# The causal mask of an attention stage moved from a TensorE matmul into two masked copies of the gate row

## Chip, cores and metric

One core of a Trainium2 chip runs the whole program in one launch. The metric is device time in microseconds (us) from the first to the last instruction; lower is better. The kernel before takes 1215.36 us, the median of three runs (1215.21 to 1215.37).

## What is computed

One decoder layer for a sequence of 1024 positions and a width of 1024, all float32. The input is modulated, projected, and mixed by two groups of heads: eight "FoX" heads of width 64 (causal softmax attention with a forget gate) and four retention heads of width 128. An output projection, a layer norm, a gated MLP with a short convolution and a second layer norm follow. The change concerns the FoX heads:

```python
cum = jnp.cumsum(log_f, axis=1).transpose(0, 2, 1)        # per head, over positions
s = jnp.einsum('bhqd,bhkd->bhqk', qi, kh) * scale          # qi: one block of 128 queries
s = s + ci[..., None] - cum[:, :, None, :]
s = jnp.where(key_pos[None, :] <= q_pos[:, None], s, -jnp.inf)
p = jax.nn.softmax(s, axis=-1)
o = jnp.einsum('bhqk,bhkd->bhqd', p, vh)
```

The term `ci` is the same for a whole row of the softmax and drops out. What remains is a row of gate sums, one value per key, added to every query's scores, and the causal mask, which matters only in the 128x128 block on the diagonal: key blocks past it are not computed at all.

## The kernel before

**Numbers in pieces.** Float32 products are made of three TensorE matmuls: an operand is split into a high part (a cast on ScalarE, ACT) and a low part (a subtraction on VectorE, DVE), and high x high, high x low and low x high are accumulated in PSUM.

**The stages.** First come the conditioning rows, the retention heads and the v projection of the FoX heads; their instructions are put in order by a scheduler that works with a timeline. This block also computes the gate sums: log_forget at chunk 8 of the 16 chunks of the v projection, cum_forget at chunk 14, cum_store (which writes the sums to the DRAM tensor cum_d) at chunk 15. Then comes the attention stage, 281 to 476 us of the span, with its order of work written out by hand; then the output projection, the layer norm, the MLP.

**The attention stage.** A loop of 64 steps runs over 8 heads x 8 query blocks; the names in the profile carry head and block, so S3_5 is block 5 of head 3. Step (h, i) does this:

- TensorE (PE) makes the scores of query block i against keys 0 to 128(i+1), negated, in PSUM tile ps: one matmul for the high part of q (L796) and one for the low part (L797) per cut of up to 512 keys, both against ks. In the last cut a third matmul (L800) multiplies a bfloat16 identity by a bfloat16 mask (0, or a big number above the diagonal) and so adds the mask to the diagonal block.
- DVE adds the gate row nb (a copy of head h's row of cum_d on all 128 partitions, 512 KB, loaded at L753) and takes the row minimum in the same instruction (L802). ACT takes exp(min - S) with its row sum (L809), DVE the reciprocal (L812), GpSimd (POOL) multiplies S by it (L813).
- Three steps later (LAG) PE transposes S block by block (L835), ACT casts the high part (L841), DVE subtracts for the low part (L842). Four steps later, every other step, PE multiplies by v (L851); ACT and DVE add the result into mixF (L857, L858).
- The q and k projection of the next head is spread over steps 3 to 7 and 0 to 2 (PE L765 to L767, then ACT and DVE L771 to L781, which write qh, ks and ql).

fox_alloc (L750) takes the tiles of a head at step 3 of the head before, nb among them: from the pool X (16 buffers of 4 KB per partition) for the first two heads and from the pool VM after that, where the v tiles of finished heads come free.

**The weights of a head.** fox_w (L636) takes two new tiles of X, loads w_qk of head h into a raw tile (512 KB), casts the high part in one ACT instruction of 128x1024 (L641) and subtracts the low part in two DVE instructions of 128x512 (L644). It is called at step 4, for the head after the next.

**Other work in the stage.** w_out is split in pieces: loaded (park), cast (L990), subtracted (L997) and stored to DRAM (wod, SP L1003); in head 7 the split halves come back as sixteen loads of 512 KB (wo, SP L1009). SyncE (SP) also copies parts of w_down inside DRAM (td, L1112). All these transfers are issued by SP in one order; where one of them must wait for an engine, those behind it in SP's order wait too. Adding DMAs (a DMA that adds to its destination) are issued from POOL's queue; before, the MLP alone has them (L1106).

## Time and profile before

| What | Value |
| --- | --- |
| median of three runs | 1215.36 us (1215.21 to 1215.37) |
| span of the profiled execution | 1214.8 us |
| busy in that span: PE, PEld (weight loads) | 1198.3 us (99%), 1002.4 us (83%) |
| busy: DVE, ACT, POOL | 910.9 us (75%), 653.9 us (54%), 229.0 us (19%) |
| granted clock of TensorE | 0.999 |
| the 64 mask matmuls (L800) | 14.7 us busy, 230 ns each in the median |
| the 64 minima (L802) | 47.4 us busy, 741 ns each in the mean |
| the 8 loads of nb, 512 KB each | 5.1 us from issue to landing in the median |

A row of the profile reads: line, engine, operation, output tile <- input tiles, shape, count, then busy time and the mean of one, then how long the engine had been idle before these instructions and which instruction ended that idle time. In the timeline a row begins with start and length in us. PE's matmuls are pipelined, so that lengths overlap: the next one starts before the last has ended. SPq is SP's queue of DMA issues. The profiled execution has a span of 1214.8 us, 0.56 less than the median of the runs.

### The profile page before, as it was taken

Reading aid. Unit: us, or ns where it says so; the run is one execution under the profiler, and the core shown is the slowest. Engines: PE = TensorE matmul, PEld = TensorE weight load, DVE = VectorE, ACT = ScalarE, POOL = GpSimd, SP = SyncE. Lnnn points to the kernel's source line nnn. Section 1 sums busy time; section 2 is a strip of 40 time slices with the busy share of each in tenths; the row PEclk is TensorE's granted clock in tenths of the full one; section 3 lists DMA queues with packets and bytes.
Section 4 is the critical chain, followed back from the end, with each engine's and each line's share of the span. In section 5 each row is a group of like instructions: output and inputs, shape, how many; then the busy total and the mean of one; then the engine's idle time right before and its main releaser. Section 6 shows DMA issues by size and latency. Waiting matters only on the chain.

```text
span 1214.8 us, 17196 instructions
## 1 busy us (share of the span) xinstructions
PE 1198.3 (99%) x6005; PEld 1002.4 (83%) x6005; DVE 910.9 (75%) x1757; ACT 653.9 (54%) x1201; POOL 229.0 (19%) x274
## 2 busy tenths in 40 slices
PE   8999999999999999999999999999999999999997
PEld 6888888997888888888888888888888888888875
DVE  7847747766888887456988778787787876886586
ACT  6635444345777766567755545455454565543452
POOL 0015335012333333000021323211000010000021
PEclk9999999999999999999999999999999999999999
DMA  9523444605575658223268887776554489875751
GB/s 358 227 87 122 139 148 143 202 32 175 164 222 164 203 171 335 96 77 115 87 178 204 193 223 185 171 184 175 152 139 128 148 249 297 321 243 178 248 181 69
DMA packets 94279, 216.57 MB, mean 178 GB/s; under 512 B 10784, under 2 KB 17136, under 8 KB 94192
## 3 DMA queue, kind: packets, MB, share of 16 engines
q1 hardware_dynamic: 81520, 192.40, 46.0%
q0 software_dynamic: 12672, 23.07, 11.8%
q8 instruction: 47, 0.77, 0.3%
q14 instruction: 40, 0.33, 0.1%
HBM read 173.45 MB, written 76.59 MB: 206 GB/s over the span
## 4 chain that ended last, share of the span: by engine, by line
PE 87%; DMA 5%; DVE 4%; ACT 1%; issue 1%; SPq 0%; POOL 0%; DVEq 0%; ACTq 0%; POOLq 0%
PE rp L152 11%; PE dX L1489 7%; PE uX L1264 7%; PE uX L1263 7%; PE uX L1265 7%; PE dZ L1489 5%; PE uY L1263 5%; PE uY L1265 5%; PE uY L1264 5%; PE vp L152 4%; PE pv L851 3%; DMA ada<-in_ada_dram 3%; PE pt L835 2%; PE op L189 2%; PE op L191 2%; PE op L190 2%
## 5 line engine op out<-in xcount | busy, mean ns | idle before, releaser
L152 PE MATMUL rp<-wr,hhi 128*128 128x512 f32 x400 | 127.9, 401 | 0.0
L1475 DVE TENSOR_TENSOR dl<-dr,dh 128x1024 fp32r<-128x1024 f32 x66 | 80.3, 1237 | 36.3 <-ACT dh L1463 35.1
L813 POOL TENSOR_TENSOR S<-S,dn 128x128 f32<-128x128 f32 (+3 forms) x64 | 73.5, 1154 | 151.7 <-DVE dn L812 130.1
L1463 ACT CAST dh<-dr 128x1024 fp32r<-128x1024 f32 x58 | 59.6, 1051 | 65.7 <-DMA dr<-td 35.5
L1106 POOL DMA_DIRECT2D sd<-gd x22 | 18.1, 823 | 398.5 <-DMA sd<-y 227.2
L152 PEld LDWEIGHTS rp<-wr,hhi 128*128 128x128 f32 x400 | 71.6, 189 | 12.7
L152 PE MATMUL rp<-wr,hlo 128*128 128x512 f32 x200 | 78.6, 393 | 0.0
L1489 PE MATMUL dX<-dh 128*128 128x512 f32 x176 | 68.5, 389 | 0.8 <-DVE ds L1641 0.8
L1489 PE MATMUL dX<-dl,dh 128*128 128x512 f32 x176 | 68.5, 389 | 0.0
L1489 PE MATMUL dX<-dh,dl 128*128 128x512 f32 x176 | 68.5, 389 | 0.0
L1278 ACT COPY u<-uX 128x512 f32<-128x512 f32 x44 | 25.8, 586 | 70.3 <-PE uX L1265 70.3
L152 DVE CUSTOM_DVE_ANT_0 ada<-ada,csb,bcol 128x1024 f32<-128x1024 f32 x46 | 60.1, 1309 | 3.0 <-DMA ada<-in_ada_dram 3.0
L842 DVE TENSOR_TENSOR pt<-pt,pt 128x512 fp32r<-128x512 f32 (+2 forms) x96 | 50.7, 549 | 10.2 <-ACT pt L841 9.1
L809 ACT ACTIVATE S<-S,mn 128x128 f32<-128x128 f32 (+3 forms) x64 | 49.9, 779 | 11.1 <-DVE mn L802 10.5
L765 PE MATMUL qk<-hhi,wqh 128*128 128x512 f32 x128 | 54.8, 428 | 0.4 <-DVE pt L828 0.4
L767 PE MATMUL qk<-hhi,wql 128*128 128x512 f32 x128 | 51.9, 405 | 0.0
L1489 PE MATMUL dZ<-dh 128*128 128x512 f32 x132 | 51.6, 391 | 0.0
L1489 PE MATMUL dZ<-dl,dh 128*128 128x512 f32 x132 | 51.4, 389 | 0.0
L1489 PE MATMUL dZ<-dh,dl 128*128 128x512 f32 x132 | 51.4, 389 | 0.0
L841 ACT CAST pt<-pt 128x512 fp32r<-128x512 f32 (+2 forms) x96 | 44.1, 478 | 13.4 <-PE pt L835 12.1
L189 PE MATMUL op<-wo,mxs 128*128 128x512 f32 x128 | 51.1, 399 | 0.0
L802 DVE CUSTOM_DVE_ANT_0 S<-ps,nb 128x128 f32<-128x128 f32 (+3 forms) x64 | 47.4, 741 | 4.2 <-PE ps L800 3.5
(1049 smaller groups left out, 3661.7 us busy)
## 6 DMA issues: line engine op xcount, KB each, us to landing
ada<-in_ada_dram SPq DMA_DIRECT2D x48, 512.0 KB, 3.7
td<-in_w_down_dram SPq DMA_DIRECT2D x44, 256.0 KB, 5.4
wa<-in_w_up_dram SPq DMA_DIRECT2D x22, 512.0 KB, 4.7
wb<-in_w_up_dram SPq DMA_DIRECT2D x22, 512.0 KB, 4.1
gd<-y SPq DMA_DIRECT2D x22, 512.0 KB, 3.2
sd<-y SPq DMA_DIRECT2D x44, 256.0 KB, 3.4
dr<-sd SPq DMA_DIRECT2D x44, 256.0 KB, 3.9
dr<-td SPq DMA_DIRECT2D x44, 256.0 KB, 4.3
```

Source lines behind the costliest of these rows:

```text
L152: order[key] = fn(*args, **kw)
L189: mm(pt, ahi, whi, start=start, stop=False)
L765: nc.tensor.matmul(pt, whi[:, j, :], hhi[j][:, sl], start=(j == 0), stop=False)
L767: nc.tensor.matmul(pt, wlo[:, j, :], hhi[j][:, sl], start=False, stop=(j == ND - 1))
L813: nc.gpsimd.tensor_tensor(out=Ssb[:, :span], in0=Ssb[:, :span], in1=den.to_broadcast([P, span]), op=ALU.mult,)
L842: nc.vector.tensor_tensor(out=dl, in0=src, in1=f(dh), op=ALU.subtract)
L1263: nc.tensor.matmul(pt, whi, bh, start=start, stop=False, skip_group_check=True)
L1264: nc.tensor.matmul(pt, whi, bl, start=False, stop=False, skip_group_check=True)
L1265: nc.tensor.matmul(pt, wlo, bh, start=False, stop=stop, skip_group_check=True)
L1463: nc.scalar.copy(hi, raw)
L1475: nc.vector.tensor_tensor(out=lo, in0=raw, in1=f(hi), op=ALU.subtract)
L1489: nc.tensor.matmul(pt, w_[:, 0, q], m_[:, 1, :], start=start and n_ == 0, stop=stop and n_ == 2, skip_group_check=True)
```

## The change

The mask matmul and its two bfloat16 tiles are gone; the mask is a float32 tile of 128x128. Each head has two copies of its gate row, nb*h*_0 for the even query blocks and nb*h*_1 for the odd ones. After its load, an adding DMA on POOL's queue adds the mask to four of the eight 128-key blocks of a copy: the even blocks of copy 0, the odd ones of copy 1. Block i of copy i%2 is thus right for step (h, i), where it lies on the diagonal. For step (h, i+2), which uses the same copy, block i lies below the diagonal and must be free of the mask: after the minimum of step i (for i below 6) SP loads that block anew from cum_d, 64 KB. That makes 48 such reloads, 16 adding DMAs and 8 more loads of nb.

For the second copy there must be room. The weights of a head now lie in two tiles of X that are used by all heads: fox_load takes the raw tile at step 6, for the head after the next, and fox_w casts and subtracts a quarter of it (128x256) at each of the steps 0 to 3, behind the projection that reads the quarter for the last time. cum_forget moves from chunk 14 to 12, cum_store from 15 to 13, and the load of head 1's raw weights stays at chunk 14.

```diff
--- before.py
+++ after.py
@@ -79,16 +79,14 @@
 
     ident = cp.tile([P, P], F32, tag="ident", name="ident")
     make_identity(nc, ident)
-    identb = cp.tile([P, P], BF16, tag="identb", name="identb")
-    nc.vector.tensor_copy(identb, ident)
     epsc = cp.tile([P, 1], F32, tag="epsc", name="epsc")
     nc.vector.memset(epsc, LN_EPS)
     ones = cp.tile([P, P], F32, tag="ones", name="ones")
     nc.vector.memset(ones, 1.0)
-    maskb = cp.tile([P, P], BF16, tag="maskb", name="maskb")
-    nc.gpsimd.memset(maskb, 0.0)
+    mask = cp.tile([P, P], F32, tag="mask", name="mask")
+    nc.gpsimd.memset(mask, 0.0)
     nc.gpsimd.affine_select(
-        out=maskb, in_=maskb, pattern=[[-1, P]], compare_op=ALU.is_ge,
+        out=mask, in_=mask, pattern=[[-1, P]], compare_op=ALU.is_ge,
         fill=BIG, base=0, channel_multiplier=1,
     )
     tri = cp.tile([P, P], F32, tag="tri", name="tri")
@@ -633,18 +631,19 @@
             v_load(2 * (c - 2))
 
 
-    def fox_w(h):
-        raw = slot("R", [P, ND, P], F32, f"wqkr{h}")
-        nc.sync.dma_start(raw, w_qk[h])
-        whi = slot("X", [P, ND, P], F32R, f"wqh{h}")
-        wlo = slot("X", [P, ND, P], F32R, f"wql{h}")
-        nc.scalar.copy(whi, raw)
-        for q in range(2):
-            sl = slice(4 * q, 4 * q + 4)
-            nc.vector.tensor_tensor(
-                out=wlo[:, sl, :], in0=raw[:, sl, :], in1=f(whi[:, sl, :]), op=ALU.subtract
-            )
-        return whi, wlo
+    wraw = {}
+
+    def fox_load(h):
+        wraw[h] = slot("R", [P, ND, P], F32, f"wqkr{h}")
+        nc.sync.dma_start(wraw[h], w_qk[h])
+
+    def fox_w(h, part):
+        sl = slice(2 * part, 2 * part + 2)
+        raw, (whi, wlo) = wraw[h], wqk
+        nc.scalar.copy(whi[:, sl, :], raw[:, sl, :])
+        nc.vector.tensor_tensor(
+            out=wlo[:, sl, :], in0=raw[:, sl, :], in1=f(whi[:, sl, :]), op=ALU.subtract
+        )
 
 
     L = cp.tile([P, NT, FH], F32, tag="L", name="L")
@@ -733,14 +732,18 @@
         if q in (2, 10):
             mod_rows(q // 8)
         if q == 3:
-            w = fox_w(0)
+            wqk = [slot("X", [P, ND, P], F32R, f"wq{n}") for n in "hl"]
+            fox_load(0)
+            for part in range(4):
+                fox_w(0, part)
         if q == 8:
             Lp = log_forget()
+        if q == 12:
+            cum = cum_forget(Lp)
+        if q == 13:
+            cum_store(cum)
         if q == 14:
-            cum = cum_forget(Lp)
-            nw = fox_w(1)
-        if q == 15:
-            cum_store(cum)
+            fox_load(1)
 
     blk.__exit__(None, None, None)
 
@@ -749,13 +752,23 @@
 
     def fox_alloc(h):
         t = {n: slot("X", [P, S], F32R, f"{n}{h}") for n in ("qh", "ql", "ks")}
-        t["nb"] = slot("X" if h < 2 else "VM", [P, S], F32, f"nb{h}")
-        pins["nb"] = nc.sync.dma_start(t["nb"], bass.AP(
-            tensor=cum_d.tensor, offset=cum_d.offset + h * S, ap=[[0, P], [1, S]]))
+        t["nb"] = []
+        for p in range(2):
+            nb = slot("X" if h < 2 or p == 0 else "VM", [P, S], F32, f"nb{h}_{p}")
+            pins["nb"] = nc.sync.dma_start(nb, cum_rows(h, 0, S))
+            nc.gpsimd.dma_start(
+                nb.rearrange("p (k t q) -> p k t q", t=2, q=P)[:, :, p, :],
+                mask.unsqueeze(1).to_broadcast([P, NT // 2, P]),
+                accum_op=ALU.add, max_dma_last_dim=2048)
+            t["nb"].append(nb)
         return t
 
-    def fox_proj(h, w, T, t, part):
-        whi, wlo = w
+    def cum_rows(h, k0, k1):
+        return bass.AP(tensor=cum_d.tensor, offset=cum_d.offset + h * S + k0,
+                       ap=[[0, P], [1, k1 - k0]])
+
+    def fox_proj(h, T, t, part):
+        whi, wlo = wqk
         qh, ql, ks = T["qh"], T["ql"], T["ks"]
         sl = slice(t * 512, (t + 1) * 512)
         if part == 0:
@@ -781,7 +794,7 @@
             nc.vector.tensor_copy(ql[64:, sl], f(ql[:64, sl]))
 
     def fox_scores(h, i, T, beside=None):
-        qh, ql, ks, nb = T["qh"], T["ql"], T["ks"], T["nb"]
+        qh, ql, ks, nb = T["qh"], T["ql"], T["ks"], T["nb"][i % 2]
         span = (i + 1) * P
         tag = "S" if i % 2 == 0 else "R" if h < FH - 1 else "VM"
         Ssb = slot(tag, [P, S], F32, f"S{h}_{i}")
@@ -792,17 +805,14 @@
         qs = slice(i * P, (i + 1) * P)
         pt = bank2(f"ps{h}_{i}")
         for k0, k1 in cuts:
-            last = k0 <= i * P < k1
             nc.tensor.matmul(pt[:, k0:k1], qh[:, qs], ks[:, k0:k1], start=True, stop=False)
-            nc.tensor.matmul(pt[:, k0:k1], ql[:, qs], ks[:, k0:k1],
-                             start=False, stop=not last)
-            if last:
-                nc.tensor.matmul(pt[:, i * P:(i + 1) * P], identb, maskb,
-                                 start=False, stop=True)
+            nc.tensor.matmul(pt[:, k0:k1], ql[:, qs], ks[:, k0:k1], start=False, stop=True)
         pins["min"] = nc.vector.tensor_tensor_reduce(
             out=Ssb[:, :span], in0=pt[:, :span], in1=nb[:, :span], scale=1.0, scalar=3e38,
             op0=ALU.add, op1=ALU.min, accum_out=mn,
         )
+        if i + 2 < NT:
+            nc.sync.dma_start(nb[:, qs], cum_rows(h, i * P, (i + 1) * P))
         if beside is not None:
             beside()
         den = small([P, 1], f"dn{h}_{i}")
@@ -1118,15 +1128,15 @@
     LOADS = {0: (4, 5), 1: (6, 7), 2: (0, 1), 3: (2, 3)}
     T = {0: fox_alloc(0)}
     for part in range(4):
-        fox_proj(0, w, T[0], 0, part)
-    fox_proj(0, w, T[0], 1, 0)
+        fox_proj(0, T[0], 0, part)
+    fox_proj(0, T[0], 1, 0)
     Sb = {}
 
     def proj(h, i):
         if i < 3:
-            fox_proj(h, w, T[h], 1, i + 1)
+            fox_proj(h, T[h], 1, i + 1)
         elif h + 1 < FH:
-            fox_proj(h + 1, w, T[h + 1], *divmod(i - 3, 4))
+            fox_proj(h + 1, T[h + 1], *divmod(i - 3, 4))
 
     for s_ in range(FH * NT + LAG + 1):
         h, i = divmod(s_, NT)
@@ -1136,15 +1146,12 @@
                     for half in range(2):
                         mixF[h // 4, half] = slot("VM", [P, 2, 512], F32, f"mixF{h // 4}_{half}")
             if i == 3:
-                w = nw
                 if h + 1 < FH:
                     T[h + 1] = fox_alloc(h + 1)
             if i >= 3:
                 proj(h, i)
             k = LOWS.get(s_)
             Sb[s_] = fox_scores(h, i, T[h], None if k is None else lambda: park_low(k))
-            if i == 4 and h + 2 < FH:
-                nw = fox_w(h + 2)
             if i == 6:
                 down_base(h)
             if k is not None:
@@ -1163,6 +1170,10 @@
             fox_turn(r // NT, r % NT, Sb.pop(r))
         if h < FH and not (i >= 3):
             proj(h, i)
+        if i < 4 and h + 1 < FH:
+            fox_w(h + 1, i)
+        if i == 6 and h + 2 < FH:
+            fox_load(h + 2)
         if h == FH - 1 and i == 0:
             for q in range(2):
                 op_load(q)
```

Three places where the order of the instructions shows it. First DVE at the start of the stage, head 0, from the end of the first projection (CAST ql0, which the second listing leaves out) to the third minimum (block 2). Before (ISA S0_i is the minimum of block i, its second row writes the accumulated value; MEMSET clears a tile for the transposes):

```order
L781 CAST ql0_3144<-ql0_3144 64x512
L828 MEMSET pt0_0_0_0_3279 128x128
L828 MEMSET pt0_0_0_1_3280 128x128
L802 ISA S0_0_3188,mn0_0_3189<-ps0_0_3190,nb0_3146 128x128
L802 ISA mn0_0_3189 128x1
L802 ISA S0_1_3208,mn0_1_3209<-ps0_1_3210,nb0_3146 128x256
L802 ISA mn0_1_3209 128x1
L812 RECIPROCAL dn0_0_3195<-dn0_0_3195 128x1
L812 RECIPROCAL dn0_1_3215<-dn0_1_3215 128x1
L802 ISA S0_2_3229,mn0_2_3230<-ps0_2_3231,nb0_3146 128x384
L802 ISA mn0_2_3230 128x1
```

And now:

```order
L644 TENSOR_TENSOR wql_2585<-wqkr1_3092,wqh_2584 128x256 x2
L810 ISA S0_0_3190,mn0_0_3191<-ps0_0_3192,nb0_0_3144 128x128
L810 ISA mn0_0_3191 128x1
L838 MEMSET pt0_0_0_0_3291 128x128
L810 ISA S0_1_3212,mn0_1_3213<-ps0_1_3214,nb0_1_3147 128x256
L810 ISA mn0_1_3213 128x1
L838 MEMSET pt0_0_0_1_3292 128x128
L822 RECIPROCAL dn0_0_3197<-dn0_0_3197 128x1
L838 MEMSET pt0_1_0_0_3354 128x128
L838 MEMSET pt0_1_0_1_3355 128x128
L822 RECIPROCAL dn0_1_3219<-dn0_1_3219 128x1
L644 TENSOR_TENSOR wql_2585<-wqkr1_3092,wqh_2584 128x256 x2
```

Four quarters of the weight subtraction for head 1 (wql, two to a row) now stand in front of the minima of blocks 0 and 2 (that of block 2 follows right behind the last row); the minimum of block 1 reads the other copy, nb0_1.

Second, SP in head 7, the issues of the wo loads (and g_row, a row for the output projection). Before:

```order
L1009 DMA wo0_5_5492<-wod5_3138 128x1024
L1170 DMA g_row0_5486<-gates_98 128x1024
L1009 DMA wo1_5_5494<-wod5_3138 128x1024
L1009 DMA wo0_6_5547<-wod6_3139 128x1024
L1009 DMA wo1_6_5549<-wod6_3139 128x1024
L1009 DMA wo0_7_5551<-wod7_3140 128x1024
L1009 DMA wo1_7_5553<-wod7_3140 128x1024
L1009 DMA wo0_0_5592<-wod0_3133 128x1024
L1009 DMA wo1_0_5594<-wod0_3133 128x1024
L1009 DMA wo0_1_5596<-wod1_3134 128x1024
L1009 DMA wo1_1_5598<-wod1_3134 128x1024
```

And now, with the reloads of nb7_0 and nb7_1 (128x128) among them, each of which waits for the minimum of its step:

```order
L1019 DMA wo0_5_5534<-wod5_3136 128x1024
L815 DMA nb7_0_5292<-cum_d_2396 128x128
L1181 DMA g_row0_5528<-gates_96 128x1024
L1019 DMA wo1_5_5536<-wod5_3136 128x1024
L815 DMA nb7_1_5295<-cum_d_2396 128x128
L1019 DMA wo0_6_5589<-wod6_3137 128x1024
L1019 DMA wo1_6_5591<-wod6_3137 128x1024
L1019 DMA wo0_7_5593<-wod7_3138 128x1024
L1019 DMA wo1_7_5595<-wod7_3138 128x1024
L815 DMA nb7_0_5292<-cum_d_2396 128x128
L1019 DMA wo0_0_5634<-wod0_3131 128x1024
L1019 DMA wo1_0_5636<-wod0_3131 128x1024
```

The wo loads stood in one row; now groups of four to one stand between reloads.

Third, POOL in head 1, from the multiply of block 1 on. Before there are multiplies alone:

```order
L813 TENSOR_TENSOR S1_1_3475<-S1_1_3475,dn1_1_3482 128x256
L813 TENSOR_TENSOR S1_2_3530<-S1_2_3530,dn1_2_3537 128x384
L813 TENSOR_TENSOR S1_3_3579<-S1_3_3579,dn1_3_3587 128x512
L813 TENSOR_TENSOR S1_4_3627<-S1_4_3627,dn1_4_3636 128x640
L813 TENSOR_TENSOR S1_5_3658<-S1_5_3658,dn1_5_3668 128x768
```

And now, with the two adding DMAs for head 2:

```order
L823 TENSOR_TENSOR S1_1_3484<-S1_1_3484,dn1_1_3491 128x256
L823 TENSOR_TENSOR S1_2_3541<-S1_2_3541,dn1_2_3548 128x384
L759 DMA nb2_0_3583<-mask_75 128x4x128
L823 TENSOR_TENSOR S1_3_3596<-S1_3_3596,dn1_3_3604 128x512
L759 DMA nb2_1_3586<-mask_75 128x4x128
L823 TENSOR_TENSOR S1_4_3646<-S1_4_3646,dn1_4_3655 128x640
L823 TENSOR_TENSOR S1_5_3670<-S1_5_3670,dn1_5_3680 128x768
```

Each adding DMA stands in front of the multiply of the next step and can be issued only when the copy that it adds to has landed.

## Prediction

> **What bounds the kernel now.** I read the page's engine shares and its chain first, then the windows of the attention stage (281 to 476 us, the 64 score steps, where nearly all of the diff acts), then the mask's own lines.
>
> ```profile
> PE 1198.3 (99%) x6005; PEld 1002.4 (83%) x6005; DVE 910.9 (75%) x1757; ACT 653.9 (54%) x1201; POOL 229.0 (19%) x274
> ...
> PE 87%; DMA 5%; DVE 4%; ACT 1%; issue 1%; SPq 0%; POOL 0%; DVEq 0%; ACTq 0%; POOLq 0%
> ```
>
> The same in the stage and in head 7 (columns: busy of PE, weight loads, DVE, ACT, POOL; granted clock; DMA share; GB/s):
>
> ```profile
> 281.00:476.00 195.00, 193.42 (x1173) 162.34 (x1173) 162.86 (x449) 141.80 (x319) 71.53 (x63) 1.00 0.62 202
> ...
> 455.00:476.00 21.00, 21.00 (x137) 17.90 (x136) 19.18 (x60) 16.04 (x40) 9.62 (x9) 1.00 0.97 376
> ```
>
> PE idles 195.00 - 193.42 = 1.6 us in the stage: it is the bound, and time taken off its queue comes off the end, as long as no other engine is late in its place. DVE is busy for 162.86, 84%: a head lasts 24.4 us, of which DVE has 4.0 free. The DMA engines have room except in head 7, where they are at 0.97. The clock is 1.00 throughout and has no part in this.
>
> **The mask matmuls leave.** 64 matmuls of 128 columns and 64 weight loads go.
>
> ```profile
> L800 PE MATMUL ps<-maskb,identb x64: 219/230/232, 281.3 to 474.6; 128*128 128x128 bf16 x64
> ```
>
> Its 230 ns is a pipelined length, not a price: 64 x 0.23 = 14.7 us is out of reach. I price it by pairs, the same successor with and without the mask ahead of it. Three pv matmuls, with the mask (first two rows) and without:
>
> ```profile
> 464.58 0.23 PE L800 MATMUL ps<-maskb,identb 128*128 128x128 bf16 x1
> 464.62 0.60 PE L851 MATMUL pv<-pt,V 128*128 128x256 f32 x3
> ...
> 470.14 0.51 PE L851 MATMUL pv<-pt,V 128*128 128x256 f32 x3
> ```
>
> From the mask's start to the end of the third pv: 0.04 + 0.60 = 0.64 us; without it 0.51. The mask costs 0.13. Before a transpose:
>
> ```profile
> 366.50 0.28 PE L797 MATMUL ps<-ks,ql 128*128 128x256 f32 x1
> 366.62 0.23 PE L800 MATMUL ps<-maskb,identb 128*128 128x128 bf16 x1
> 366.69 0.39 PE L835 MATMUL pt<-ident,S 128*128 128x128 f32 x2
> ...
> 353.02 0.28 PE L797 MATMUL ps<-ks,ql 128*128 128x256 f32 x1
> 353.14 0.60 PE L835 MATMUL pt<-ident,S 128*128 128x128 f32 x4
> ```
>
> From the ql matmul's start to the transpose's: 0.19 with, 0.12 without, so 0.07. A transpose follows in some steps, pv or qk in others; I take 0.107, a little over the middle (0.10) because the longer matmuls follow more often. **64 x 0.107 = -6.8 us**, between 64 x 0.07 = -4.5 and 64 x 0.13 = -8.3. All of it lies on the path, because PE does.
>
> The Trainium skill, "TensorE: Matmul & The Clock Gate", section "Back-to-back issue gap", gives about 81 ns for each 128-column matmul in a stream of weight loads and matmuls; by it an estimate is 64 x 0.081 = 5.2 us, and the whole sum would come out 1.6 us higher. The pairs lie on both sides of it, 0.07 and 0.13.
>
> **The mask comes by DMA instead.** Sixteen adding DMAs on POOL's queue, each of 256 KB in 512-byte pieces. The stage has none now; the kernel's later ones show the price of an issue:
>
> ```profile
> L1106 POOL DMA_DIRECT2D td<-td x22: 812/978/2427, 634.3 to 831.5; - x22
> ...
> DMA to landing us min/median/max: 4.0/6.0/11.3
> ```
>
> Two per head, 0.8 us each (2.4 at worst), on an engine that is busy 71.53 of 195: 1.6 us of the 15 that it has free per head. POOL also waits at such an issue until the copy has landed, and the normalising multiply of the next step is queued behind. How much that multiply can wait:
>
> ```profile
> L813 POOL TENSOR_TENSOR S<-S,dn 128x128 f32<-128x128 f32 (+3 forms) x64 | 73.5, 1154 | 151.7 <-DVE dn L812 130.1 <-PE ps L800 10.8 <-DVE pt L828 9.2
> L809 ACT ACTIVATE S<-S,mn 128x128 f32<-128x128 f32 (+3 forms) x64 | 49.9, 779 | 11.1 <-DVE mn L802 10.5
> L812 DVE RECIPROCAL dn<-dn 128x1 f32<-128x1 f32 x64 | 10.0, 157 | 10.4 <-ACT S L809 9.4
> ```
>
> The transposes of a block come three steps after its scores, 3 x 24.4/8 = 9.1 us; exponential, reciprocal and multiply take 0.78 + 0.16 + 1.15 = 2.1 of them in the mean. So **0**, at most 1 us in sum.
>
> **The reloads.** 48 of 64 KB on SP, each issued when the minimum of its step has ended, and needed by the minimum two steps on. What a landing takes (kind, count, KB, median us from issue), and the tightest usual window, from the minimum of step 0 of head 4 to that of step 2:
>
> ```profile
> td<-in_w_down_dram SPq DMA_DIRECT2D x44, 256.0 KB, 5.4
> wod<-park SPq DMA_DIRECT2D x32, 256.0 KB, 2.5
> wo<-wod SPq DMA_DIRECT2D x16, 512.0 KB, 10.2
> nb<-cum_d SPq DMA_DIRECT2D x8, 512.0 KB, 5.1
> ...
> mr<-mixR SPq DMA_DIRECT2D x2, 256.0 KB, 3.2
> ...
> cum_d<-cumT SPq DMA_DIRECT2D x1, 32.0 KB, 1.8
> ```
>
> ```profile
> 378.58 0.08 DVE L802 DVE_READ_ACCUMULATOR2_ANT mn<- 128x1 f32 x1
> ...
> 382.94 0.49 DVE L802 CUSTOM_DVE_ANT_0 S<-ps,nb 128x384 f32<-128x384 f32 x1
> ```
>
> 382.94 - 378.66 = 4.3 us. By size a reload lies between 1.8 and 3.2, so with its issue it just fits: I take 2.5 and **+0.4 us** over heads 1 to 6 for the few that find a td or nb transfer ahead (0 to 7 if 5.4 were the rule). SP's waits for a minimum hold the td, park and wod transfers behind them. SP does such waiting already while PE stays full:
>
> ```profile
> SPq L1003 <- ACT park L990: 52.0, 11, 10.0
> ```
>
> **Head 7.** Its wo loads of 512 KB are issued ahead and drain for 10.2 us each in the median, at 0.97 of the DMA engines. The reloads now stand among them in SP's order, so a reload issued behind four of them lands about 5.6 us later (512 KB at the 376 GB/s of the window are 1.39). Two of the windows there:
>
> ```profile
> 465.46 0.08 DVE L802 DVE_READ_ACCUMULATOR2_ANT mn<- 128x1 f32 x1
> ...
> 469.26 0.07 DVE L802 DVE_READ_ACCUMULATOR2_ANT mn<- 128x1 f32 x1
> 469.60 0.94 DVE L802 CUSTOM_DVE_ANT_0 S<-ps,nb 128x768 f32<-128x768 f32 x1
> ...
> 471.54 1.08 DVE L802 CUSTOM_DVE_ANT_0 S<-ps,nb 128x896 f32<-128x896 f32 x1
> ```
>
> 469.60 - 465.54 = 4.1 us from step 3 to step 5, and 471.54 - 469.33 = 2.2 from step 4 to step 6. Against some 2 + 5.6 the reloads for steps 5 to 7 come 3 to 6 us late. But their transposes too come three steps later, and PE has out-projection matmuls to bring forward: **+0.5 us** (0 to 3).
>
> **The start of head 0.** The cumulative sums are stored two chunks earlier, because the copies must now be loaded and then masked before their first use. The last narrow v projection, the store, the first load and the second minimum:
>
> ```profile
> 272.14 0.28 PE L152 MATMUL vp<-wv,hlo 128*128 128x256 f32 x1
> ...
> 272.88 0.53 SPq L725 DMA_DIRECT2D cum_d<-cumT  x1
> 274.77 0.33 SPq L753 DMA_DIRECT2D nb<-cum_d  x1
> ...
> 281.81 0.43 DVE L802 CUSTOM_DVE_ANT_0 S<-ps,nb 128x256 f32<-128x256 f32 x1
> ```
>
> With the store about 5.8 us sooner (an estimate: two chunks of the v projection), the even copy is loaded at 274.77 - 5.8 + 5.1 = 274 and masked, 4 to 6 us later, by 280: in time. The odd one takes the buffer of the last v weights, held until 272.4; loaded at 277.5, masked it is ready at 281.5 to 283.5, against 281.81. Behind that minimum stand two of the new weight subtractions, then the minimum of step 2. **+0.8 us** (0.4 to 2.5).
>
> **The weights of the next head in four parts.** Two subtractions of 512 columns become four of 256. The row of before, and the nearest row for the new width:
>
> ```profile
> L644 DVE TENSOR_TENSOR wql<-wqkr,wqh 128x512 fp32r<-128x512 f32 x12 | 7.8, 688 | 1.7 <-ACT wqh L641 1.2 <-POOL S L813 0.5
> L641 ACT CAST wqh<-wqkr 128x1024 fp32r<-128x1024 f32 x6 | 6.3, 1052 | 0.6 <-DMA wqkr<-in_w_qk_dram 0.6
> L1039 DVE TENSOR_TENSOR mxs<-mixF,mxs 128x256 fp32r<-128x256 f32 x6 | 2.4, 420 | 1.5 <-ACT mxs L1038 1.5
> L1038 ACT CAST mxs<-mixF 128x256 fp32r<-128x256 f32 x6 | 2.2, 401 | 1.7 <-PE op L191 1.7
> ```
>
> 4 x 0.42 - 2 x 0.688 = +0.3 us of DVE per head, and 4 x 0.40 - 1.05 = +0.55 of ACT, beside 4.0 us that DVE has free. In return step 4 is relieved, where cast and subtractions stood in the chain in one piece. These balance: **0** (-1 to +1).
>
> A subtraction with both inputs in SBUF can be held by POOL's multiply. The parking subtraction, of the same size, shows it:
>
> ```profile
> L997 DVE TENSOR_TENSOR park<-park,park x16: 673/689/1167, 288.7 to 448.1; 128x512 fp32r<-128x512 f32 x16
> ```
>
> Most take 0.689, the worst 1.167, +0.48. Were each of 28 pieces held so in POOL's 37% of the time (71.53 of 195), that is 28 x 0.37 x 0.48 = 5.0 us of DVE, against 2.1 for the 12 now: +0.4 per head, still inside the 4.0 free. The Trainium skill, "SBUF — State Buffer", section "Who interferes with whom", has the rule that a DVE instruction with two SBUF inputs and a GpSimd instruction that reads SBUF exclude each other for the whole instruction. It speaks against more and smaller subtractions; by it alone the sum would be up to 2.9 us higher, if none of that DVE time were covered.
>
> **Sum.** -6.8 + 0 + 0.4 + 0.5 + 0.8 + 0 = -5.1 against the profiled execution's span of 1214.8: 1209.7. The median of the runs, 1215.36, is 0.56 above the span, so **1210.3 us**.
>
> **The rivals.** A measurement here tells 0.2%, 2.4 us, from no change: faster ends at 1212.9, slower begins at 1217.8.
>
> 1. *The forecast*, 1210.3: 0.55.
> 2. *More comes free.* PE's 1.6 us of idle in the stage goes too, because step 4 is no longer blocked by one lump of weight work, and no reload shows: -6.8 - 1.6 + 0.4 = -8.0, 1207.4. For it: the subtraction waits for its cast (1.2 of 1.7 us, the row above). Against: most of PE's waits lie elsewhere. 0.13.
> 3. *Another engine becomes the bound.* DVE at 84%, its work up and the steps shorter. If half of the steps end on DVE or ACT, half of 6.8 shows: -3.4 + 0.4 + 0.5 + 0.8 = -1.7, 1213.7, within the bound. For it: DVE is at 19.18 of 21.00 in head 7. Against: 4.0 us free in each other head. 0.17.
> 4. *Slower: the reloads land late in every head.* Transfers from SP drain in order; if a reload meets a td, nb or wqk transfer ahead as a rule, it lands after 5.4 us plus its own share, 6 to 7, against windows of 4.3 (the row above) to about 5 at steps 0, 3 and 4. DVE then stands some 2 us at each, with the low-part subtractions for the transposes queued behind it, and PE waits for those. At 1.5 us net per head, 7 x 1.5 = 10.5, and 2 in head 7: -6.8 + 0.8 + 10.5 + 2 - 1.5 (idle that PE already has) = +5.0, 1220.4. It decides from a landing of 4.3 us on. For it: td's 5.4. Against: DMA at 0.62 in the stage, and wod's 2.5. 0.15.
>
> That the change does not do what it says is out: the order of its instructions has 64 matmuls and 64 weight loads fewer on PE.
>
> Faster 0.55 + 0.13 = 0.68, the same 0.17, slower 0.15. The range must leave out 0.2 at most: it goes from 1206.8, below case 2, to 1216.0, past case 3 with the upper ends of head 0 (+1.7) and some of head 7; case 4 stays outside.
>
> **What would show it.** Right: in the attention stage PE is as full as before and ends about 6 us sooner; reloads land 2 to 3 us after issue; the minimum waits for a DMA only in head 7 and once or twice in head 0. Wrong: DVE's waits for nb add up to over 7 us (case 4), PE's idle in the stage grows to 5 us with no DMA behind it (case 3), or POOL's multiply waits for its own mask DMA and transposes wait for it. Wrong in size: the step behind the mask's place is shortened by less than 0.07 or more than 0.13 us.

## Result: slower by 1.8%, and the profile after

The changed kernel takes 1237.63 us (median of four runs, 1235.95 to 1238.72) against 1215.36: a ratio of 1.0178, 95% interval 1.0165 to 1.019. The profiled execution has a span of 1235.6 us, 20.8 more than before.

The page's busy times and its chain:

```profile
PE 1201.6 (97%) x5941; PEld 1002.1 (81%) x5941; DVE 921.6 (75%) x1772; ACT 656.6 (53%) x1225; POOL 252.2 (20%) x290
...
PE 85%; DMA 8%; DVE 4%; issue 1%; ACT 1%; SPq 1%; POOL 0%; DVEq 0%; ACTq 0%; POOLq 0%
```

PE fell from 99% to 97% busy; DMA rose from 5% to 8% of the chain that ended last. The stage, now 281 to 507 us, and its last head (busy of PE, weight loads, DVE, ACT, POOL; clock; DMA share; GB/s):

```profile
281.00:507.00 226.00, 206.85 (x1163) 170.79 (x1164) 178.21 (x477) 146.68 (x346) 90.66 (x78) 0.98 0.78 230
476.00:507.00 31.00, 28.99 (x171) 24.01 (x170) 22.57 (x63) 17.41 (x44) 7.78 (x8) 1.00 0.85 310
```

PE stands idle for 19.2 us of the stage, where it stood for 1.6 of 195 before. Who PE waited for:

```profile
PE qk L778 <- DVE mixF L868: 5.5, 4, 2.1
PE pt L845 <- DVE mixF L868: 3.3, 3, 1.8
PE pv L861 <- DVE pt L852: 2.8, 1, 2.8
PE pt L845 <- DVE ks L790: 2.3, 4, 1.3
PE ps L808 <- DVE mn L810: 2.1, 2, 1.5
PE pt L845 <- POOL S L823: 1.1, 2, 0.7
```

Nearly all of it is DVE, though DVE itself is 79% busy. For the most part DVE passes a wait on: it works in order, and stands in front of a minimum whose copy of the gate row is not ready. So the row to look for is what DVE and POOL wait for. The minima (L810) wait for the reloads, and under "issue" (idle time with no releaser in the profile) the longest, 4.3 us, is for the second mask of head 0, which follows below:

```profile
DVE S L810 <- DMA nb<-cum_d: 8.0, 5, 2.6
DVE S L810 <- issue: 5.7, 4, 4.3
```

The adding DMAs on POOL, and what POOL had idled for ahead of them:

```profile
L759 POOL DMA_DIRECT2D nb<-mask x16: 1287/1312/1492, 273.5 to 462.2; - x16
...
  DMA nb<-cum_d: 50.9, 11
  PE ps L809: 7.5, 1
  issue: 7.0, 2
...
DMA to landing us min/median/max: 4.5/6.1/9.6
```

The 7.0 us of "issue" have no releaser here either, and the 7.5 us put down to PE is of the same kind, as the timeline of POOL at the start of head 0 shows (start, length, idle time before):

```profile
273.52 1.49 POOL L759 DMA_DIRECT2D nb<-mask  x1 [20.64 <-DMA nb<-cum_d]
282.54 1.31 POOL L759 DMA_DIRECT2D nb<-mask  x1 [7.53 <-PE ps L809]
287.29 1.29 POOL L759 DMA_DIRECT2D nb<-mask  x1 [3.44 <-issue]
```

The first took 8.8 us to land, at 282.28, the second 4.5, at 287.04: each next one is issued a quarter of a microsecond after the one before has landed, although its own copy had been there long since (that of the second at 277.25). Of the fifteen adding DMAs that follow another, six are issued so, 0.26 to 0.32 us after the landing of the one before; the other nine come later, and the profile puts them down to the landing of a load. The minimum of block 1 waited for the second mask and began at 287.16, 5.4 us later than before.

The reloads: landing in the trace as a whole, then two places of the chain where a minimum waits for one:

```profile
DMA to landing us min/median/max: 2.8/4.0/9.5
```

```profile
290.70 6.56 DMA nb<-cum_d
...
297.40 0.82 DVE S L810
...
481.48 8.46 DMA nb<-cum_d
...
490.10 0.82 DVE S L810
```

The second is in head 7, where the reload stands among the wo loads.

### The profile page after: what moved, and what is told of

It is laid out like the page before. It is cut to its first block, busy times and chain, and to the rows that moved or that the text cites. A ratio compares the mean times of both kernels' runs of the same rounds, so it can differ in the third digit from the quotient of the medians.

```text
span 1235.6 us, 17288 instructions
## 1 busy us (share of the span) xinstructions
PE 1201.6 (97%) x5941; PEld 1002.1 (81%) x5941; DVE 921.6 (75%) x1772; ACT 656.6 (53%) x1225; POOL 252.2 (20%) x290
## 4 chain that ended last, share of the span: by engine, by line
PE 85%; DMA 8%; DVE 4%; issue 1%; ACT 1%; SPq 1%; POOL 0%; DVEq 0%; ACTq 0%; POOLq 0%
PE rp L150 11%; PE dX L1500 10%; PE dZ L1500 7%; PE uX L1275 6%; PE uX L1274 6%; PE uX L1276 6%; PE uY L1274 5%; PE uY L1275 5%; PE uY L1276 5%; PE vp L150 4%; DMA ada<-in_ada_dram 3%; DMA nb<-cum_d 2%; PE op L189 2%; PE op L188 2%; PE op L187 2%; PE pv L861 2%
## 5 line engine op out<-in xcount | busy, mean ns | idle before, releaser
L1486 DVE TENSOR_TENSOR dl<-dr,dh 128x1024 fp32r<-128x1024 f32 x66 | 80.4, 1239 | 37.7 <-ACT dh L1474 36.5
L823 POOL TENSOR_TENSOR S<-S,dn 128x128 f32<-128x128 f32 (+3 forms) x64 | 78.8, 1270 | 87.5 <-DVE dn L822 74.9
L810 DVE CUSTOM_DVE_ANT_0 S<-ps,nb 128x128 f32<-128x128 f32 (+3 forms) x64 | 48.1, 752 | 20.1 <-DMA nb<-cum_d 8.0
L845 PE MATMUL pt<-ident,S 128*128 128x128 f32 x288 | 46.8, 278 | 7.3 <-DVE mixF L868 3.3
L779 PE MATMUL qk<-hlo,wqh 128*128 128x512 f32 x128 | 53.4, 417 | 0.0
L861 PE MATMUL pv<-pt,V 128*128 128x256 f32 x320 | 48.1, 287 | 4.2 <-DVE pt L852 2.8
```

The lines of the kernel that those rows point to most:

```text
L779: nc.tensor.matmul(pt, whi[:, j, :], hlo[j][:, sl], start=False, stop=False)
L823: nc.gpsimd.tensor_tensor(out=Ssb[:, :span], in0=Ssb[:, :span], in1=den.to_broadcast([P, span]), op=ALU.mult,)
L861: nc.tensor.matmul(pv[:, :256], V2[h][:, kb, :], pts[kb // 4][u][:, kb % 4, :], start=(kb == 0 and u == 0), stop=(kb == nkb - 1 and u == 1),)
L1486: nc.vector.tensor_tensor(out=lo, in0=raw, in1=f(hi), op=ALU.subtract)
```

## The experiments

Three theories came out of this. **1**: the reloads land too late. **2**: the adding DMAs hold POOL, either (2a) because POOL waits for the load of a copy, or (2b) because one adding DMA can't be issued until another has landed, or (2c) because their traffic slows everything. **3**: the weights in quarters cost it. All times are medians in us; the kernel before, run beside them, took 1215.8 to 1216.2. The ratio to it stands behind a time where it decides, with its interval.

### What the matmuls were worth, and what each part costs

**a_no_mask**, on the kernel before (no mask at all):

```diff
-            nc.tensor.matmul(pt[:, k0:k1], ql[:, qs], ks[:, k0:k1],
-                             start=False, stop=not last)
-            if last:
-                nc.tensor.matmul(pt[:, i * P:(i + 1) * P], identb, maskb,
-                                 start=False, stop=True)
+            nc.tensor.matmul(pt[:, k0:k1], ql[:, qs], ks[:, k0:k1], start=False, stop=True)
```

> The kernel before without its mask matmuls; nothing takes their place, so this leaves the causal mask of the diagonal blocks out. It measures the gain on TensorE alone. By the price of the prediction (0.107 us each) 1215.4 - 6.8 = 1208.6 us. If the mask matmul costs only the 0.04 us to the next start, 1212.8. If DVE or ACT ends the steps in its place, 1213 or more.

1212.41, ratio 0.9970 (0.9959 to 0.9981): -3.6 us. From the first minimum to the last, before and without mask:

```profile
281.56:474.89 193.33, 191.75 (x1160) 160.75 (x1160) 161.44 (x445) 141.70 (x318) 70.42 (x63) 1.00 0.61 200
```

```profile
283.60:473.62 190.02, 186.44 (x1102) 159.05 (x1101) 161.97 (x446) 142.08 (x318) 69.89 (x63) 1.00 0.63 206
```

PE is busy 5.3 us less, 0.083 for each of 64 matmuls (over the whole program 1192.7 against 1198.3 us, 0.088 each), but the stage is only 3.3 us shorter: PE's idle time went from 1.6 to 3.6.

**b_no_reload**, **c_no_mask_dma** and **d_neither**, on the changed kernel: b takes out the first pair of lines, c the second statement, d both.

```diff
-        if i + 2 < NT:
-            nc.sync.dma_start(nb[:, qs], cum_rows(h, i * P, (i + 1) * P))
...
-            nc.gpsimd.dma_start(
-                nb.rearrange("p (k t q) -> p k t q", t=2, q=P)[:, :, p, :],
-                mask.unsqueeze(1).to_broadcast([P, NT // 2, P]),
-                accum_op=ALU.add, max_dma_last_dim=2048)
```

> The changed kernel without the 48 reloads (blocks masked for one step stay masked for the later ones: that part of the computation is wrong by it). Theory 1, the reloads land too late (median 4.0 us, 8 to 9.5 in head 7, not 2.5): nearly all of the loss but the start of head 0 goes, about 1217 us (1215 to 1220). Theory 2, the masking DMAs on POOL's queue and the second loads cost it: still over 1228. Theory 3, the weights in quarters keep DVE and ACT late: still over 1228, with PE idle in heads 1 to 6.

> The changed kernel without the 16 adding DMAs (no mask at all; the reloads stay and write what is there already). Theory 1, late reloads: the start of head 0 comes back (about 5 us) and the reloads meet less traffic, but most stays: 1228 to 1233 us. Theory 2, masking DMAs: about 1217. Theory 3, quarters: 1232 or more.

> The changed kernel without reloads and without adding DMAs (no mask): what is left of the change is the missing matmuls, eight more loads of the gate row and the weights in quarters. Theories 1 and 2 together: 1208 to 1211 us, as the kernel before without mask matmuls plus at most 2. Theory 3: 1215 or more.

b 1233.39, c 1224.88, d 1215.36 (ratio 0.9992, 0.9983 to 1.0002). So the adding DMAs alone cost 1233.4 - 1215.4 = 18.0 us, the reloads alone 9.5; together they cost 22.3, some 5 less than the sum. Theory 1 as the main cause falls, theory 2 leads; c, at 1224.88, lies in no theory's range, because each has a share. And d is 3 us above a: there is something in theory 3.

How an adding DMA costs time, in b, where no reload disturbs. POOL in head 3, the PE row that follows, and the landings of the first two:

```profile
370.42 1.29 POOL L759 DMA_DIRECT2D nb<-mask  x1 [2.64 <-DVE mixF L866]
371.24 1.90 POOL L821 TENSOR_TENSOR S<-S,dn 128x256 f32<-128x256 f32 x2
380.27 1.31 POOL L759 DMA_DIRECT2D nb<-mask  x1 [7.13 <-DVE pt L850]
381.08 1.57 POOL L821 TENSOR_TENSOR S<-S,dn 128x512 f32<-128x512 f32 x1
387.92 1.31 POOL L759 DMA_DIRECT2D nb<-mask  x1 [5.27 <-DMA td<-in_w_down_dram]
388.74 3.20 POOL L821 TENSOR_TENSOR S<-S,dn 128x640 f32<-128x640 f32 x2
```

```profile
390.57 1.11 PE L843 MATMUL pt<-ident,S 128*128 128x128 f32 x4 [4.17 <-POOL S L821]
```

```profile
DMA to landing us min/median/max: 9.5/9.5/9.5
...
DMA to landing us min/median/max: 7.3/7.3/7.3
```

370.42 + 9.53 = 379.95, and the next is issued at 380.27; 380.27 + 7.34 = 387.61, and the next at 387.92. Behind each stands a multiply. That of block 4 was ready at 380.35 (end of its reciprocal) and started at 388.74; its transposes started 0.06 us after it ended, and PE had idled for 4.17 us.

### Queue or traffic: the reloads

**f_reload_act**, on c_no_mask_dma:

```diff
-            nc.sync.dma_start(nb[:, qs], cum_rows(h, i * P, (i + 1) * P))
+            nc.scalar.dma_start(nb[:, qs], cum_rows(h, i * P, (i + 1) * P))
```

> As c_no_mask_dma (reloads, no adding DMAs, no mask: 1224.9 us), but the 48 reloads are issued on ACT's queue and not on SP's. Theory 1a, a reload stands in line behind the transfers that SP issued ahead of it: landings fall from a median of 4 to below 3 us and the 9.5 us of late reloads go to 3 or less, 1216 to 1219. Theory 1b, the DMA engines' traffic alone sets the landing, whichever queue issues: within 2 us of 1224.9.

1238.42: 13.5 us slower than c, which neither theory had. DVE's waits for a reload, c and then f (total, times, longest):

```profile
DVE S L806 <- DMA nb<-cum_d: 11.0, 6, 3.5
```

```profile
DVE S L806 <- DMA nb<-cum_d: 22.8, 13, 3.0
```

The landing's median is 3.8 us against 3.6, the longest 7.7 against 9.6; but over 5 us took 13 of the 32 reloads whose landing is in the trace, in c 8 of 36. On another queue the reloads land no sooner, so that they stand in line behind SP's earlier transfers (1a) falls. What is left is traffic (1b), but not at the time that 1b gave, within 2 us of c. One reading: in c SP waits at each reload for its minimum, and the td, park and wod transfers behind it wait too; in f no reload holds them, and the traffic is less spread out. This is argued from the order of the queues, not tried. A rival was not tried either: each issue takes 0.33 us in ACT's own order, ahead of the exponential of its step, 16 us in all, and the exponential starts 0.75 us behind its minimum in the mean, in c 0.45. But DVE's waits for reloads alone grew by 22.8 - 11.0 = 11.8 us, which speaks against this rival.

### What POOL waits for

**j_mask_later**, on b_no_reload: the adding DMAs for head h+1 are issued behind the multiplies of steps 5 and 6 of head h.

```diff
+            if i in (5, 6) and h + 1 < FH:
+                with tc.issue_after(pins["mul"].ins):
+                    fox_mask(T[h + 1]["nb"][i - 5], i - 5)
```

> As b_no_reload (adding DMAs, no reloads: 1233.4 us), but the two adding DMAs for the next head stand on POOL's queue behind the multiplies of steps 5 and 6, when both copies have long landed. Theory 2a, POOL waits for a copy's load and the multiplies behind it are late: 1220 or less but for head 0. Theory 2b, an adding DMA of 512 pieces can't be issued until the one before has landed, and POOL waits for that: the second still holds the multiply of step 7; some of the loss stays, 1222 to 1228. Theory 2c, the traffic of the adding DMAs itself slows the rest: still over 1230.

1277.31, 44 us slower than b: far above the ranges of 2a and 2b, and "over 1230", as 2c had it, for another reason than 2c's. No multiply is late now, but the two masks of a head land one after the other, 4.2 to 10.9 us each, and the first minima of every head wait for them:

```profile
DVE S L814 <- DMA nb<-mask: 49.1, 12, 6.5
```

So 2a is not the whole: with the copies long landed, the second still waits for the first. The early place of the change's own order had at least hidden that.

**k_mask_pieces** and **n3_halves**, on b_no_reload: each adding DMA as four of 128 pieces of 512 bytes, or as two of 256.

```diff
+            for k in range(NT // 2):
+                nc.gpsimd.dma_start(
+                    nb.rearrange("p (k t q) -> p k t q", t=2, q=P)[:, k, p, :], mask,
+                    accum_op=ALU.add, max_dma_last_dim=2048)
```

> As b_no_reload (1233.4 us), but each adding DMA is made as four of 64 KB, 128 pieces each; places in POOL's order as before. Theory 2b, only so many pieces fit in flight (more than 768, as the six of 128 pieces in the MLP stage show, fewer than 1024): the four of one copy are issued without a wait for a landing, the second copy's follow sooner, 1222 to 1228. Theory 2a or 2c: within 2 us of 1233.4, or slower by the 6 more issues of 0.8 us per head on POOL.

> As b_no_reload (1233.4 us), with each adding DMA as two of 256 pieces. If a limit between 896 and 1023 pieces in flight holds POOL: three are in flight, the fourth waits for the first, and most of the gain of k_mask_pieces (1219.9) is kept: 1220 to 1226, with no issue less than three landings behind. If a second adding DMA can't follow one that is not landed because of its shape (four dimensions) and not its pieces: 1232 or more.

k 1219.88 (below the 1222 to 1228 of 2b), n3 1221.39: 13.5 and 12.0 us faster than b with the same bytes and the same number of pieces, which also rules out 2c as the main cause. POOL in k, in head 5, with the first one's landing:

```profile
414.86 0.83 POOL L821 TENSOR_TENSOR S<-S,dn 128x384 f32<-128x384 f32 x1 [2.14 <-DVE pt L836]
415.63 6.23 POOL L760 DMA_DIRECT2D nb<-mask  x7
```

```profile
DMA to landing us min/median/max: 5.6/5.6/5.6
```

Seven of 128 pieces are issued some half a microsecond apart, from 415.63 to 418.90; the eighth comes at 421.49, 0.26 us after the first has landed (415.63 + 5.60 = 421.23). In n3, at the start of head 0:

```profile
273.54 2.64 POOL L760 DMA_DIRECT2D nb<-mask  x2 [20.55 <-DMA nb<-cum_d]
277.24 1.20 POOL L760 DMA_DIRECT2D nb<-mask  x1 [1.06 <-DMA nb<-cum_d]
282.66 2.53 POOL L760 DMA_DIRECT2D nb<-mask  x2 [4.22 <-issue]
...
```

```profile
DMA to landing us min/median/max: 8.9/8.9/8.9
```

Three of 256 are in flight; the fourth is issued 0.26 us after the first has landed (273.54 + 8.86 = 282.40). 7 x 128 = 896 pieces go, 8 x 128 = 4 x 256 = 2 x 512 = 1024 don't: 2b holds, with a limit between 896 and 1023 pieces of POOL's DMAs in flight. One DMA of 512 pieces leaves no room for a second. It is not a limit of bytes: in the MLP of the kernel before, six adding DMAs of 256 KB, 128 pieces of 2 KB each, are issued from 632.2 to 634.8 us without a wait, and none of them lands in under 6.4 us. Of the 18.0 us, 13.5 go with this limit. The other 4.5 (k is that far above d) are what 2a, 2c and the limit, which k still meets, have left; they were not taken apart.

**m_pieces_full**: the changed kernel, reloads and all, with k's pieces.

> The changed kernel with each adding DMA as four of 128 pieces; reloads as they are, whole computation. Theory 2b (POOL waits for a landing when over 1000 pieces would be in flight): the 13.5 us that the pieces brought without reloads come here too, 1223 to 1226 us. If reloads and masks cost the same waits, so that one hides the other: 1227 to 1232.

1232.4, just above the 1227 to 1232 that were given for waits that hide each other: of the 13.5 us only 5.2 arrive. DVE's waits for reloads stay (8.5 us, the longest 3.7; 8.0 and 2.6 in the changed kernel). Beside whole masks the reloads cost 1237.6 - 1233.4 = 4.2 us, beside masks in pieces 1232.4 - 1219.9 = 12.5: much of what they cost had stood behind the masks' waits, so mending one half of the change is worth little.

### The weights in quarters

**e_one_copy**: d_neither with one copy of the gate row per head.

```diff
-        for p in range(2):
+        for p in range(1):
```

> As d_neither (no mask, no reloads, no adding DMAs: 1215.4 us), with one copy of the gate row per head and not two: against a_no_mask (1212.4) only the weights in quarters and the earlier gate sums are left of the change. If the eight more loads cost the 3 us between the two, 1212 to 1213. If the quarters cost them, 1214.5 to 1216. The prediction had 0 for the quarters.

1214.95, ratio 0.9992 (0.9982 to 1.0001): the eight more loads cost nothing that can be told, and the quarters remain. In d ACT waits for the raw weights, the longest time at the first quarter that is cast in head 2, with the exponential of the step before behind it:

```profile
ACT wqh L643 <- DMA wqkr<-in_w_qk_dram: 8.0, 4, 5.1
```

```profile
326.93 0.40 ACT L643 CAST wqh<-wqkr 128x256 fp32r<-128x256 f32 x1 [5.06 <-DMA wqkr<-in_w_qk_dram]
327.24 1.14 ACT L813 ACTIVATE S<-S,mn 128x1024 f32<-128x1024 f32 x1
```

The load was issued at 319.49 and landed at 326.85. **n4_neither_load4** issues it two steps sooner:

```diff
-        if i == 6 and h + 2 < FH:
+        if i == 4 and h + 2 < FH:
             fox_load(h + 2)
```

> As d_neither (1215.4 us), with the raw weights of the head after the next loaded at step 4 and not at step 6. If ACT's wait for that load is what is left of the change's cost: 1212 to 1213.3 us, as a_no_mask. If the quarters themselves cost it (more instructions, other places): within 1 us of 1215.4.

1210.92, ratio 0.9958 (0.9945 to 0.9972): 4.4 us less than d, more than was expected, and ACT's wait for the load is gone. So the quarters themselves cost nothing that can be told. It is even 1.5 us below a, but the intervals of the two ratios overlap, so a gain is not shown. **p1_load4** does the same to the changed kernel alone:

> The changed kernel (1237.6 us) with the raw weights loaded at step 4, nothing else. If the waits add up: 4.5 us less as between d_neither and n4, 1233. If the adding DMAs and reloads hide the late load behind their own waits: 1235.5 to 1239.

1235.17, just under the 1235.5 to 1239 that were given for waits that hide each other: 2.5 of the 4.4 us; the rest stands behind other waits.

### The mask without small DMAs

**h_pool_copies** (whole computation): POOL adds the mask itself, and block i is copied by POOL from the other copy, in which blocks of that parity are never masked.

```diff
-            nc.sync.dma_start(nb[:, qs], cum_rows(h, i * P, (i + 1) * P))
+            nc.gpsimd.tensor_copy(nb[:, qs], T["nb"][1 - i % 2][:, qs])
...
+        view = nb.rearrange("p (k t q) -> p k t q", t=2, q=P)[:, :, p, :]
+        nc.gpsimd.tensor_tensor(out=view, in0=view,
+                                in1=mask.unsqueeze(1).to_broadcast([P, NT // 2, P]), op=ALU.add)
...
+            if i in (6, 7) and h + 1 < FH:
+                with tc.issue_after(pins["mul"].ins):
+                    fox_mask(T[h + 1]["nb"][i - 6], i - 6)
```

> The whole computation, without small DMAs: the mask is added by POOL itself (128x512, behind the multiplies of steps 6 and 7), and after the minimum of step i block i is copied from the other copy, where it is free of the mask, by POOL (128x128). Theories 1 and 2: what is left is d_neither (1215.4 us) plus some POOL time: 1214 to 1218 us. If POOL's multiplies become late by the added 2 x 1.0 + 6 x 0.4 = 4.4 us per head: 1222 or more.

1221.38, above what was expected: the second mask came too late for the minimum of step 1 of each head:

```profile
DVE S L813 <- POOL nb L766: 10.6, 12, 1.6
```

**h4_pool_earlier** puts the masks at steps 5 and 6, **h3_act_copies** does that too and leaves the restoring copies to ACT (`nc.scalar.copy`, behind the exponential).

> As h_pool_copies (1221.4 us, where the minimum of step 1 waited about 1.5 us for the second mask of its head), with the masks behind the multiplies of steps 5 and 6 instead of 6 and 7. If that wait was the loss: 1214.5 to 1218. If POOL's copies or its port were: within 1.5 us of 1221.4.

> The whole computation without small DMAs: POOL adds the mask behind the multiplies of steps 5 and 6, and ACT restores block i from the other copy (128x128) behind the exponential of step i. Theory: what is left is d_neither (1215.4 us) and the ACT time, 48 copies of some 0.3 us beside 53 us that ACT has free: 1214.5 to 1217.5. If ACT is on the path in most steps (14 us in all): 1222 or more.

1216.0 (ratio 0.9999, 0.9990 to 1.0008) and 1216.52 (1.0003, 0.9994 to 1.0012): no faster than before, as d. Both still have the late load. With it at step 4:

> The whole computation: as h4_pool_earlier (mask and restoring copies on POOL, 1216.0 us), with the load at step 4. If the load was the cost: 1212.5 to 1214. If not: 1215 to 1217.

> The whole computation: as h3_act_copies (restoring copies on ACT, 1216.5 us), with the load at step 4. If the load was the cost: 1213 to 1214.5. If not: 1215.5 to 1217.5.

n1 1211.8, ratio 0.9965 (0.9953 to 0.9978); n2 1212.32, 0.9970 (0.9959 to 0.9982). Both beat both kernels, that of before by 4.1 and 3.6 us, a little more than expected, and n1 comes within 1 us of n4, which has no mask at all. In n1 POOL does more; PE never waits for it, DVE 0.8 us in the whole stage (the stage, the whole of PE's waits in it, then the mask's length):

```profile
281.00:476.00 195.00, 192.65 (x1133) 162.46 (x1131) 168.84 (x473) 144.25 (x343) 114.19 (x126) 1.00 0.68 227
```

```profile
PE pv L864 <- ACT pt L854: 1.0, 1, 1.0
PE pv L864 <- DVE pt L855: 0.5, 2, 0.3
PE op L187 <- DVE mixF L871: 0.2, 1, 0.2
```

```profile
L766 POOL TENSOR_TENSOR nb<-nb,mask x16: 1285/1296/1301, 272.5 to 450.2; 128x512 f32<-128x512 f32 x16
```

Adding the mask takes POOL 1.30 us; issuing the DMA that adds it took 1.31. **p2_reload_only** is n1 with SP's reloads in place of POOL's copies:

> The whole computation: as n1_pool_load4 (1211.8 us), but blocks are restored by the 48 reloads on SP and not by POOL's copies; the mask stays POOL's own addition. The reloads alone then cost what c_no_mask_dma was over d_neither, 9.5 us: 1219 to 1223. If their cost came from a late load or the traffic of the adding DMAs: under 1215.

1218.54, just under the range given (1219 to 1223): the reloads cost 6.7 us by themselves. DVE waits for them 9.5 us in ten places. From p2 to p1 (the same reloads and load, masks by DMA) it is 16.6 us more.

## Why the prediction was wrong

The step that failed is the one on the adding DMAs, "**0**, at most 1 us in sum". It priced their issue by a row of DMAs of 128 pieces (0.8 to 2.4 us) and their lateness by the slack of one multiply, 9.1 - 2.1 us. It named the wait for the copy's load, but not that the next adding DMA waits for the one before to land. Its last list has a multiply that waits for its own mask DMA as a sign of being wrong, but no rival gave that a price or a chance. With two per head at 4.5 to 9.6 us, behind a load that lands after about 5, that wait is as long as the slack and at times longer, as block 4 of head 3 showed. The runs put 16.6 to 18 us in place of the 0, of which 13.5 go with the limit on pieces in flight and the rest was not taken apart. The trace of before had half of the evidence, six DMAs of 128 pieces issued without a wait in the MLP; no row of it showed 512 pieces.

The other terms:

- **Mask matmuls**, -6.8: measured -3.6. PE's busy time fell by 0.083 to 0.088 per matmul, inside 0.07 to 0.13 and below the 0.107 taken; the 0.081 of the Trainium skill ("TensorE: Matmul & The Clock Gate", section "Back-to-back issue gap") was nearer. So of the 3.2 us missing some 1.5 are size (6.8 - 5.3); 2.0 us went into new idle time of PE, where the term had "All of it lies on the path".
- **Reloads**, +0.4: measured +9.5 alone, +6.7 in the mended kernel. They land in 4.0 us in the median, not 2.5. Rival 4 had the late landing, with a chance of 0.15 and a price of 1.5 us per head; it came to about 1. Its reason, that transfers from SP drain in order, did not hold in f, where the reloads on another queue landed no sooner; that traffic does it is what is left, and was not tried by itself.
- **Head 7**, +0.5: from the minimum of step 3 to the last the delay grows from 19.3 to 30.6 us, with reloads that land after 8.0 to 9.5 us, but the end of the program is only 20.8 late. PE brought out-projection matmuls forward, as forecast: about 1.5 us net, within 0 to 3.
- **Start of head 0**, +0.8 (0.4 to 2.5): measured 5.4 at the second minimum. The two masks were taken as independent; they came one after the other.
- **Weights in quarters**, 0: the arithmetic of their lengths was right (0.420 us in the median), but the change moves a DMA too, and the term did not look at it: the raw load, issued at step 6 with 7.4 us to land and needed at step 0. It cost 4.4 us where nothing else hid it, outside the -1 to +1. The rule on two SBUF inputs (the Trainium skill, "SBUF — State Buffer", section "Who interferes with whom") showed no price in the 28 quarters of the stage, 426 ns in the mean, 6 above the median.

That rule may have had a price in the sixteen parking subtractions, which the prediction took as its example:

```profile
L1007 DVE TENSOR_TENSOR park<-park,park x16: 676/690/3795, 293.4 to 467.0; 128x512 fp32r<-128x512 f32 x16
```

They take 19.1 us, 13.1 before and 11.2 and 11.4 in c and d, which have no adding DMA. The longest runs from 439.12 to 442.91, beside two multiplies from 439.57 to 442.36 that an adding DMA had held up until they came in one go. This is time of DVE's own, some 6 us of the change; what it is worth on the path was not tried.

What was right: PE was the bound before, and the matmuls' time does come off, though only half of it. Without the small DMAs and with the load at step 4, n1 stands at 1211.8, near the 1210.3 forecast, but by another sum: a put the matmuls at 3.6 us, not 6.8. Relief at step 4 is not shown (n4 and a lie within noise of each other).

Open: why an adding DMA of 256 KB takes from 4.5 to 9.6 us to land, the 4.5 us of the adding DMAs beyond the limit, the overlap of some 5 us between masks and reloads, and why ACT's queue is so much worse for the reloads.

## What to carry to other kernels

Price a new DMA by rows of the same number and size of pieces, and ask for the second one in a row as well as the first. A wait on an engine's own queue costs what stands behind it there: name that instruction and its slack. Where a small tile is in SBUF already, let an idle engine add or copy it: here one POOL instruction took as long as issuing the DMA in its place.

## What the runs showed of the hardware

- POOL's adding DMAs: 896 pieces of 512 bytes were in flight (k), 1024 never; the next issue then came 0.25 to 0.32 us after the oldest had landed. An issue took 1.31 us for 512 pieces.
- A load of 64 KB in 512-byte pieces into SBUF never landed in under 2.8 us, and took 3.6 to 4.1 in the median at 217 to 236 GB/s in all.
- Issuing 48 such loads on ACT's queue and not on SP's made the kernel 13.5 us slower (f against c); the cause was not isolated.
